# Sparse attention in a decoder trunk: normalising after the product with the values instead of before it

## The chip, the cores and the metric

The kernel runs on one core of one Trainium2 chip. The metric is the time of the whole program on the device, in microseconds (us): 1126.22 us is the median of three runs of the kernel before (1125.14, 1126.22 and 1126.79).

## What is computed

The reference is a two-layer decoder trunk for 512 tokens of 1024 channels. Layer 0 projects the normed tokens once and hands the columns to two mixers: gated linear attention, and a sparse attention with an indexer. An output projection, a gated convolutional FFN, a spatial gating layer and a second FFN follow. The change lies in the sparse attention, which, with the selection of keys already made, is

```python
s = einsum('bqhd,bqkd->bqhk', qb, kg) * d ** -0.5
s = where(valid[:, :, None, :], s, -inf)
p = softmax(s, axis=-1)
o = einsum('bqhk,bqkd->bqhd', p, vg)
```

for 8 heads of 64 channels; keys and values are shared by the heads. Since the softmax divides a row by one number, dividing the row of `o` instead of the row of `p` gives the same result.

## The kernel before, in words

Everything lies transposed, channels on the 128 partitions and tokens along the free axis, except where a step says otherwise. Weights come in chunks of 128 x 1024, each split in a high and a low part (`make_chunk`, lines 132 to 150), and a full-precision product is three matmuls (`mm3`, lines 159 to 162).

Layer 0 is cut into steps, and `ORDER` (lines 29 and 30) lists them in the order in which the scheduler prefers them. A scheduler then places the instructions on the engines: each engine runs its own list strictly in order, and a later step's instruction is put into a place where the scheduler sees the engine free. Its last steps are `W0 TC0 W3 A0 W1 W2 A3 A1 A2`, after which the output projection follows.

- `weigh(b)` (W, lines 509 to 527) takes 128 queries. For each of the 8 heads: two matmuls `ps_qk` (lines 296 and 297), a masked row with its minimum on VectorE (line 520), the exponential with the row's sum on ScalarE (line 522), the reciprocal of the sum (line 523), and the row times the reciprocal, on VectorE (line 525) or on ScalarE (line 527). `SWAPPED` names the rows that change places. Block b has 128 (b + 1) keys, so the rows of W0, W1, W2 and W3 are 128, 256, 384 and 512 wide.
- `gather(b)` (A, lines 529 to 547): for every 128 keys (`st`) and each half of the heads (`e`) four transposes `pt_p` (line 538), a copy `pT` to SBUF (line 541 on ScalarE or line 543 on VectorE, `SWAPPED` again), and the product with the values, `po` (line 545). The two halves write to partitions 0 to 63 and 64 to 127 of `po`. At the end `po` is split in two parts, `bh` on ScalarE (line 444) and `bl` on VectorE (line 445). That makes 2, 4, 6 and 8 copies for A0 to A3, 20 in all.
- `out_half` (lines 559 to 571) projects: first the half from the linear attention (`ah`, `al`; 8 tiles `p_o` of 12 matmuls each, 96 in all), then the half from the sparse attention (`bh`, `bl`; another 96), after which the next norm is prepared. The first half needs nothing from W and A.

PSUM has two pools of four tiles each: `pacc` (function `acc`) for the projections, and `paux` (function `aux`). A tile of a pool takes the place of the one allocated four before it. In the kernel before, `po` is an `aux` tile and the pool `pacc` holds only projections.

Of the kernel before, what the change touches and what calls it, by code (L numbers as in the profile page):

```python
# [10 lines left out]
AF = mybir.ActivationFunctionType  # L11
ALU = mybir.AluOpType
PSUM = bass.MemoryType.PSUM

P = 128
# [14 lines left out]
         "ST0 GL0 GL3 TC1 GL2 GL1 AR GT1 GT0 GT2 GT3 W0 TC0 W3 A0 W1 W2 A3 A1 A2")  # L30
MIX_LAG = 4
SPREAD = 3
# what GpSimd does in place of VectorE; where ScalarE and VectorE change places
ON_POOL = {
# [4 lines left out]
}  # L39
SWAPPED = {  # L40
# [3 lines left out]
}  # L44


# [1 line left out]
def trunk(ctx: ExitStack, tc: tile.TileContext, I, out):  # L48
    nc = tc.nc
    V, S, G, PE = nc.vector, nc.scalar, nc.gpsimd, nc.tensor  # L50
# [22 lines left out]
    def aux(name):  # L73
        return paux.tile([P, T], F32, tag="aux", name=name)

    # ---- inputs that stay
    pg = cst.tile([P, 40], F32, name="pg")
    nc.scalar.dma_start(pg, I["gains"])
    pv = cst.tile([P, I["pv"].shape[1]], F32, name="pv")
# [1 line left out]
    x = [xpool.tile([P, T], F32, tag="x", name=f"x{d}") for d in range(KD)]  # L81
    con = cst.tile([P, 3, P], F32, name="con")
    nc.gpsimd.dma_start(con, I["con"])
    ident, cmask, gmask = con[:, 0, :], con[:, 1, :], con[:, 2, :]
# [19 lines left out]
    one = cst.tile([P, 1], F32, name="one")  # L104
# [8 lines left out]
    mhalf = cst.tile([P, 4], F32, name="mhalf")  # L113
    V.memset(mhalf, -0.5)

    # ---- weights: loaded in chunks of [128, 1024], each split into two float32r parts
    order = []
    for name, n in (("w_in", 20), ("w_o", 8), ("w_up0", 44), ("w_dn0", 24), ("w_uv", 16),
                    ("w_out", 8), ("w_up1", 44), ("w_dn1", 24)):
# [41 lines left out]
        PE.matmul(ps, wh, xl, start=False, stop=False)  # L161
        PE.matmul(ps, wl, xh, start=False, stop=stop)  # L162

    # ---- the normed stream: x * gain in two parts, and 1/rms of each token
    class Normed:
        pass

# [21 lines left out]
            n.last = q  # L189

    def residual(d, ps, step):
        """x[d] += ps, then the next norm's step on it; the last one is what all wait for."""
        with tc.high_priority() if d == KD - 1 else nullcontext():
            V.tensor_add(x[d], x[d], ps)
            step(d)
# [25 lines left out]
        S.copy(n.R, pr)  # L221

    def chan(n, name):
        """A chunk's 128 channels by all tokens, before 1/rms."""
        wh, wl = chunk()
        ps = acc(name)
        for k in range(KD):
            c = slice(k * P, (k + 1) * P)
            mm3(ps, wh[:, c], wl[:, c], n.h[k], n.l[k], k == 0, k == KD - 1)
            if k == SPREAD and n.stage == 1:  # L230
                spread(n)
        if n.stage == 0:
            stats(n)
        return ps

    def tokens(n, name):
        """Four chunks' 512 channels, by blocks of tokens, before 1/rms."""
        ps = [acc(f"{name}{b}") for b in range(NB)]
        for c in range(4):
            wh, wl = chunk()  # L240
            for b in range(NB):
                t = slice(b * P, (b + 1) * P)
                for k2 in range(2):
                    k = 2 * c + k2
                    w = slice(k2 * T, (k2 + 1) * T)
                    PE.matmul(ps[b], n.h[k][:, t], wh[:, w], start=k == 0, stop=False)  # L246
                    PE.matmul(ps[b], n.l[k][:, t], wh[:, w], start=False, stop=False)  # L247
                    PE.matmul(ps[b], n.h[k][:, t], wl[:, w], start=False, stop=k == KD - 1)  # L248
            if n.stage == 0:
                stats(n)  # L250
        return ps

    # ---- layer 0: attention
    n0 = normed()
    ps = [(acc if j < 2 else aux)(f"p_first{j}") for j in range(4)]
    for c in range(4):
# [13 lines left out]
        nc.gpsimd.dma_start(CS[i], I["rope"][i])  # L270

    def halves(ps, cs, name):
        """A tile after its rotation, in two parts."""
        t1 = slot("rope1")
        sw = slot("rope2")
        t = slot("rope3")
        V.tensor_mul(t1, ps, cs[0])
        V.stream_shuffle(out=sw, in_=ps, mask=swap)
        eng("rm" + name).tensor_mul(sw, sw, cs[1])
        eng("ra" + name).tensor_add(t, t1, sw)  # L280
        h = slot("rope4", F32R)
        l = slot("rope5", F32R)
        S.copy(h, t)
        eng("rs" + name).tensor_sub(l, t, h)
        return h, l

    def queries(ps, cs, dst, name):
        """dst[e] = head e's high part over its low part."""
        h, l = halves(ps, cs, name)
        for e, rows in enumerate((lo, hi)):  # L290
            nc.sync.dma_start(dst[e][lo].bitcast(F32), h[rows].bitcast(F32))
            nc.sync.dma_start(dst[e][hi].bitcast(F32), l[rows].bitcast(F32))

    def dots(ps, q, ks):
        """All four products of the parts."""
        PE.matmul(ps, q, ks[0], start=True, stop=False)
        PE.matmul(ps, q, ks[1], start=False, stop=True)

# [8 lines left out]
    h, l = halves(ps[0], RCS, "kk")  # L307
# [44 lines left out]
                if picked[b] == TOPK // 8:  # L352
                    V.tensor_scalar(mask[b], mask[b], 0.5 * TAKEN, NEG, op0=ALU.is_gt, op1=ALU.mult)

    # gated linear attention
    def queries_keys(i):
        ps = ps_aq if i == 0 else chan(n0, f"p_qk{i}")
        if i < 2:
# [11 lines left out]
    def lazy(name, shape, dt=F32):  # L370
        if name not in B:
            B[name] = big(name, shape, dt)
        return B[name]
# [69 lines left out]
    def split(h, l, ps):  # L443
        S.copy(h, ps)
        V.tensor_sub(l, ps, h)
# [53 lines left out]
        split(lazy("ah", [P, 4, T], F32R)[:, :, t], lazy("al", [P, 4, T], F32R)[:, :, t],  # L499
              pt.rearrange("p (h c) -> p h c", c=P))  # L500

    # sparse attention
    def heads(i):
        bq = lazy(f"bq{i // 2}", [P, 4, T], F32R)
        queries(chan(n0, f"p_bq{i}"), RCS, [bq[:, 2 * (i % 2) + e, :] for e in range(2)], f"bq{i}")

    prob = {}

    def weigh(b):
        n = P * (b + 1)  # L510
        t = slice(b * P, (b + 1) * P)
        prob[b] = pr = [(big(f"pr{b}{e}", [P, 4, T]) if b else
                         slot(f"pr{b}{e}").rearrange("p (j t) -> p j t", t=P)) for e in range(2)]
        mx = small("mx", 8)
        sm = small("sm", 8)
        for h in (0, 2, 4, 6, 1, 3, 5, 7):
            p = pr[h % 2][:, h // 2, :n]
            ps = aux(f"ps_qk{b}{h}")
            dots(ps[:, :n], B[f"bq{h // 4}"][:, h % 4, t], [k[:, :n] for k in keys[1]])
            V.tensor_tensor_reduce(out=p, in0=ps[:, :n], in1=mask[b], op0=ALU.add, op1=ALU.min,  # L520
                                   scale=-0.125, scalar=3.0e38, accum_out=mx[:, h:h + 1])
            S.activation(p, p, AF.Exp, bias=mx[:, h:h + 1], scale=-1.0, accum_out=sm[:, h:h + 1])
            V.reciprocal(sm[:, h:h + 1], sm[:, h:h + 1])
            if (h % 2) != (f"nm{b}{h}" in SWAPPED):
                V.tensor_scalar(p, p, sm[:, h:h + 1], None, op0=ALU.mult)
            else:
                S.activation(p, p, AF.Copy, scale=sm[:, h:h + 1])

    def gather(b):
        t = slice(b * P, (b + 1) * P)  # L530
        pr = prob.pop(b)
        po = aux(f"po{b}")
        for st in range(b + 1):
            pT = []
            for e in range(2):
                pt = aux(f"pt_p{b}{st}{e}")
                for j in range(4):
                    PE.transpose(pt[:, j * P:(j + 1) * P], pr[e][:, j, st * P:(st + 1) * P], ident)
                pT.append(slot("pT"))
                if bool(e) != (f"pT{b}{st}{e}" in SWAPPED):  # L540
                    S.copy(pT[e], pt)
                else:
                    V.tensor_copy(pT[e], pt)
            for e in range(2):
                PE.matmul(po[64 * e:64 * e + 64, :], tok[:, st, 0:64], pT[e], start=st == 0, stop=st == b)  # L545
        split(lazy("bh", [P, 4, T], F32R)[:, :, t], lazy("bl", [P, 4, T], F32R)[:, :, t],
              po.rearrange("p (j c) -> p j c", c=P))

    picked = [0] * NB
    # the steps of layer 0 in the order that the scheduler prefers  # L550
    steps = {"QK": queries_keys, "SC": scores, "LG": logits, "DC": decays, "BQ": heads, "AV": values,
             "ST": states, "GL": gla, "AR": gates, "GT": gate, "W": weigh, "A": gather,
             "TC": lambda i: topk((1, 2, 3), 4)}
    for name in ORDER.split():
        step = steps[name.rstrip("0123")]
# [18 lines left out]
    n1 = normed()  # L574
    out_half(B["bh"], B["bl"], True, n1)

    # ---- gated conv FFN
    def ffn(l, n, nxt, gi):
        g = [big(f"g{l}_{i}", [P, 4, T], F32R) for i in range(NJ // 2)]
        for j in range(NJ):  # L580
# [48 lines left out]
                residual(d, ps, step)  # L629

    def close(n, ps, t):
        """The last residual, final norm and store of 256 tokens."""
        with tc.high_priority():
            xd = x[KD - 1][:, t]
            V.tensor_add(xd, xd, ps)
# [5 lines left out]
            for b in range(2):  # L641
                c = slice(b * P, (b + 1) * P)
# [6 lines left out]
            prs = []  # L649
# [6 lines left out]
            R = slot("R")[:, :256]  # L656
# [10 lines left out]
    n2 = normed()  # L667
    ffn(0, n1, n2, 1)

    # ---- layer 1: spatial gating  # L670
    v = [big(f"v{b}", [P, 2, T]) for b in range(NB)]
    for hh in range(2):
        ps = tokens(n2, f"p_v{hh}")
# [6 lines left out]
    for b in range(NB):  # L680
        st = small("bst", 12, 2).rearrange("p (a s) -> p a s", s=6)
# [35 lines left out]
    for g in range(8):  # L717
        ps = chan(n2, f"p_u{g}")
# [8 lines left out]
    for d in range(KD):  # L727
        wh, wl = chunk()
        ps = acc(f"p_so{d}")
# [8 lines left out]
def _layout(inp):  # L738
    import numpy as np

    f = {k: np.asarray(v) for k, v in inp.items()}
    A = {}
    A["xT"] = f["x"][0].T.reshape(KD, P, T)

    def by_k(w):
        """[K, n] -> [128, K / 128, n]"""
        return w.reshape(w.shape[0] // P, P, w.shape[1]).transpose(1, 0, 2)

    w = f["attn_w_in"][0]
# [31 lines left out]
    A["ln_b"] = f["sgu_ln_b"]  # L781
    A["b_s"] = f["sgu_b_s"][0].reshape(1, 1024)
    A["w_s"] = f["sgu_w_s"][0].transpose(2, 0, 1)
    # constants of the shapes
    i = np.arange(P)
    le = i[:, None] <= i[None, :]
    A["con"] = np.stack([np.eye(P, dtype=np.float32),
# [31 lines left out]
```

## Time and profile before

| | us |
|---|---|
| median of three runs | 1126.22 |
| span of the profiled execution | 1124.9 |
| TensorE (PE) busy in it | 1099.9 (98%) |
| VectorE (DVE) busy | 717.1 (64%) |
| ScalarE (ACT) busy | 451.2 (40%) |
| GpSimd (POOL) busy | 100.8 (9%) |

The span runs from the first to the last instruction; the runs' median is 1.3 us longer, which is what lies around it. A busy time of PE counts a matmul until its modelled end, so matmuls that follow one another overlap by a little. A row of the timeline gives the start and the duration; where a count stands behind it, the row is several instructions.

### The profile page before, as it was taken

The page shows a single profiled execution, that of the slowest core. Times are in us where ns is not written, and L with a number is a line of the kernel's source. Part 1 is how long each engine was busy: PE and PEld are TensorE (multiplying, and loading weights), DVE is VectorE, ACT ScalarE, POOL GpSimd, SP SyncE. Part 2 cuts the span into 40 slices and gives each one's busy share as a digit, 9 for nine tenths or more (in the row PEclk, how much of TensorE's full clock was granted, in tenths as well). Part 3 has the DMA queues.
Part 4 walks back from the last instruction along what each step waited for, and adds up shares of the span by engine and source line. Part 5 has one row for each costly group of instructions (what it writes and reads, how often), then busy time and mean ns, then how long its engine had stood idle before and what let it go on. Part 6 is the DMA issues. An engine that isn't in the chain of part 4 may idle for free.

```text
span 1124.9 us, 13026 instructions
## 1 busy us (share of the span) xinstructions
PE 1099.9 (98%) x5043; PEld 893.1 (79%) x5043; DVE 717.1 (64%) x1112; ACT 451.2 (40%) x649; POOL 100.8 (9%) x71
## 2 busy tenths in 40 slices
PE   8997999999999999999999999999999999999997
PEld 6875767487888888888888888888888888888886
DVE  5799789667777777753333385766777777753222
ACT  6452249144444444432222333435444444433221
POOL 1454240040000000000000000120000000000001
PEclk9998999999999999999999999999999999999999
DMA  6615120122222332223333523222233322233322
GB/s 225 187 38 150 57 68 9 38 94 94 94 94 95 103 102 95 94 85 103 99 94 108 169 75 113 76 94 94 94 96 104 100 94 94 94 103 87 101 85 75
DMA packets 34925, 108.86 MB, mean 97 GB/s; under 512 B 4160, under 2 KB 6480, under 8 KB 34864
## 3 DMA queue, kind: packets, MB, share of 16 engines
q1 hardware_dynamic: 33536, 104.87, 29.4%
q10 hardware_dynamic: 1040, 2.27, 0.7%
q8 instruction: 39, 0.64, 0.2%
q0 software_dynamic: 288, 0.90, 0.2%
q14 instruction: 22, 0.18, 0.0%
HBM read 101.73 MB, written 2.10 MB: 92 GB/s over the span
## 4 chain that ended last, share of the span: by engine, by line
PE 92%; DVE 5%; ACT 1%; issue 1%; DMA 0%; POOL 0%; POOLq 0%; SPq 0%; DVEq 0%; ACTq 0%
PE p_up L161 14%; PE p_up L162 14%; PE p_up L160 14%; PE p_dn L162 7%; PE p_dn L161 7%; PE p_dn L160 7%; PE po L545 1%; PE p_v L246 1%; PE p_so L160 1%; PE p_so L161 1%; PE p_u L160 1%; PE p_v L248 1%; PE p_u L161 1%; PE p_so L162 1%; PE p_u L162 1%; PE p_v L247 1%
## 5 line engine op out<-in xcount | busy, mean ns | idle before, releaser
L160 PE MATMUL p_up<-xh,h_w_up 128*128 128x512 f32 x704 | 274.3, 390 | 0.7 <-ACT xh L173 0.7
L161 PE MATMUL p_up<-xl,h_w_up 128*128 128x512 f32 x704 | 274.0, 389 | 0.6 <-DVE xl L174 0.6
L162 PE MATMUL p_up<-xh,l_w_up 128*128 128x512 f32 x704 | 273.9, 389 | 0.0
L160 PEld LDWEIGHTS p_up<-xh,h_w_up 128*128 128x128 f32 x704 | 132.1, 188 | 28.3 <-ACT xh L173 1.1
L161 PEld LDWEIGHTS p_up<-xl,h_w_up 128*128 128x128 f32 x704 | 132.1, 188 | 28.3 <-DVE xl L174 0.9
L162 PEld LDWEIGHTS p_up<-xh,l_w_up 128*128 128x128 f32 x704 | 132.1, 188 | 27.4
L161 PE MATMUL p_dn<-g,h_w_dn 128*128 128x512 f32 (+1 forms) x374 | 140.9, 377 | 0.0
L160 PE MATMUL p_dn<-g,h_w_dn 128*128 128x512 f32 (+1 forms) x374 | 140.9, 377 | 0.0
L162 PE MATMUL p_dn<-g,l_w_dn 128*128 128x512 f32 (+1 forms) x374 | 140.9, 377 | 0.0
L149 DVE TENSOR_TENSOR l_w_dn<-raw_w_dn,h_w_dn 128x1024 fp32r<-128x1024 f32 (+1 forms) x48 | 54.5, 1136 | 107.7 <-ACT h_w_dn L148 107.6
L148 ACT CAST h_w_up<-raw_w_up 128x1024 fp32r<-128x1024 f32 x88 | 92.7, 1054 | 62.5 <-PE p_up L161 47.7
L587 DVE TENSOR_TENSOR a<-p_up,R 128x512 f32<-128x512 f32 x88 | 60.5, 688 | 84.5 <-PE p_up L162 79.3
L149 DVE TENSOR_TENSOR l_w_up<-raw_w_up,h_w_up 128x1024 fp32r<-128x1024 f32 x87 | 106.5, 1224 | 9.4 <-ACT h_w_up L148 7.0
L148 ACT CAST h_w_dn<-raw_w_dn 128x1024 fp32r<-128x1024 f32 (+1 forms) x48 | 47.2, 983 | 147.8 <-PE p_dn L161 143.4
L160 PEld LDWEIGHTS p_dn<-g,h_w_dn 128*128 128x128 f32 x374 | 70.4, 188 | 13.0
L161 PEld LDWEIGHTS p_dn<-g,h_w_dn 128*128 128x128 f32 x374 | 70.4, 188 | 12.9
L162 PEld LDWEIGHTS p_dn<-g,l_w_dn 128*128 128x128 f32 x374 | 70.4, 188 | 12.8
L599 ACT CAST g<-c 128x512 fp32r<-128x512 f32 x44 | 27.3, 621 | 116.8 <-DVE c L596 116.8
L589 ACT ACTIVATE c<-a,pv 128x512 f32<-128x512 f32 x88 | 71.7, 815 | 2.9 <-DVE a L587 2.3
L592 DVE SCALAR_TENSOR_TENSOR c<-a,pv,c 128x510 f32<-128x510 f32 x88 | 65.9, 749 | 3.0
L590 DVE SCALAR_TENSOR_TENSOR c<-a,pv,c 128x511 f32<-128x511 f32 x88 | 65.6, 745 | 1.8 <-ACT c L589 1.8
L595 ACT ACTIVATE c<-c 128x512 f32<-128x512 f32 x44 | 27.8, 632 | 82.6 <-DVE c L592 82.6
(259 smaller groups left out, 1620.2 us busy)
## 6 DMA issues: line engine op xcount, KB each, us to landing
raw_w_up<-in_w_up SPq DMA_DIRECT2D x88, 512.0 KB, 3.3
raw_w_dn<-in_w_dn SPq DMA_DIRECT2D x32, 512.0 KB, 3.4
raw_w_in<-in_w_in SPq DMA_DIRECT2D x16, 512.0 KB, 3.6
raw_w_uv<-in_w_uv SPq DMA_DIRECT2D x16, 512.0 KB, 3.4
raw_w_dn<-in_w_dn SPq DMA_DIRECT2D x16, 384.0 KB, 3.1
raw_w_o<-in_w_o SPq DMA_DIRECT2D x8, 512.0 KB, 3.3
raw_w_out<-in_w_out SPq DMA_DIRECT2D x8, 512.0 KB, 3.4
x<-in_xT SPq DMA_DIRECT2D x8, 256.0 KB, 5.1
```

What stands on the lines that cost most here:

```text
L148: S.copy(h[:, :cols], raw[:, :cols])
L149: eng(name).tensor_sub(l[:, :cols], raw[:, :cols], h[:, :cols])
L160: PE.matmul(ps, wh, xh, start=start, stop=False)
L161: PE.matmul(ps, wh, xl, start=False, stop=False)
L162: PE.matmul(ps, wl, xh, start=False, stop=stop)
L246: PE.matmul(ps[b], n.h[k][:, t], wh[:, w], start=k == 0, stop=False)
L587: V.tensor_mul(a, ps, n.R)
L589: S.activation(cc, a, AF.Identity, bias=conv_b(l, m), scale=conv_w(l, m, 2))
L590: V.scalar_tensor_tensor(cc[:, 1:], a[:, :T - 1], conv_w(l, m, 1), cc[:, 1:], op0=ALU.mult, op1=ALU.add)
L592: V.scalar_tensor_tensor(cc[:, 2:], a[:, :T - 2], conv_w(l, m, 0), cc[:, 2:], op0=ALU.mult, op1=ALU.add)
L595: S.activation(c[0], c[0], AF.Silu)
L599: S.copy(gh, c[1])
```

## The change

- `weigh` leaves the probabilities as the exponentials. The 32 reciprocals of one column become 4 of eight columns, and the 32 multiplications of a row are gone.
- `gather` takes `po` from `acc` instead of `aux`. At its end GpSimd spreads the eight reciprocals over 512 columns (`wide`), PE transposes that in four pieces (`pt_rs`), ScalarE copies it to SBUF (`Rsum`), VectorE multiplies `o = po * Rsum`, and the split reads `o`.
- The copies `pT` go to VectorE for `e = 0` and to ScalarE for `e = 1`. `SWAPPED` is gone.

The diff without its removed comments:

```diff
-SWAPPED = {
...
-    prob = {}
+    prob, sums = {}, {}
...
             S.activation(p, p, AF.Exp, bias=mx[:, h:h + 1], scale=-1.0, accum_out=sm[:, h:h + 1])
-            V.reciprocal(sm[:, h:h + 1], sm[:, h:h + 1])
-            if (h % 2) != (f"nm{b}{h}" in SWAPPED):
-                V.tensor_scalar(p, p, sm[:, h:h + 1], None, op0=ALU.mult)
-            else:
-                S.activation(p, p, AF.Copy, scale=sm[:, h:h + 1])
+        V.reciprocal(sm, sm)
+        sums[b] = sm
...
         pr = prob.pop(b)
-        po = aux(f"po{b}")
+        rs = sums.pop(b)
+        po = acc(f"po{b}")
...
-                if bool(e) != (f"pT{b}{st}{e}" in SWAPPED):
+                if e:
                     S.copy(pT[e], pt)
                 else:
                     V.tensor_copy(pT[e], pt)
...
+        wide = slot("wide")
+        G.tensor_copy(wide.rearrange("p (h c) -> p h c", c=64), rs[:, :, None].to_broadcast([P, 8, 64]))
+        prs = aux(f"pt_rs{b}")
+        for j in range(4):
+            PE.transpose(prs[:, j * P:(j + 1) * P], wide[:, j * P:(j + 1) * P], ident)
+        R = slot("Rsum")
+        S.copy(R, prs)
+        o = slot("o")
+        V.tensor_mul(o, po, R)
         split(lazy("bh", [P, 4, T], F32R)[:, :, t], lazy("bl", [P, 4, T], F32R)[:, :, t],
-              po.rearrange("p (j c) -> p j c", c=P))
+              o.rearrange("p (j c) -> p j c", c=P))
```

The order of the instructions moves too. PE before, where A0 ends and W1 begins (`po0` is A0's product, `ps_qk1x` are W1's rows, `p_o1` and `p_o2` belong to the first half of the output projection):

```order
L160 MATMUL p_o1_1951<-ah_1447,h_w_o_0_1377 128x512
L545 MATMUL po0_1637<-pT_1643,tok_439 64x512
L296 MATMUL ps_qk10_1662<-key10_422,bq0_675 128x256
L545 MATMUL po0_1637<-pT_1650,tok_439 64x512
L297 MATMUL ps_qk10_1662<-key11_423,bq0_675 128x256
L296 MATMUL ps_qk12_1669<-key10_422,bq0_675 128x256
L297 MATMUL ps_qk12_1669<-key11_423,bq0_675 128x256
L296 MATMUL ps_qk14_1676<-key10_422,bq1_768 128x256
L297 MATMUL ps_qk14_1676<-key11_423,bq1_768 128x256
L161 MATMUL p_o1_1951<-al_1448,h_w_o_0_1377 128x512
L162 MATMUL p_o1_1951<-ah_1447,l_w_o_0_1378 128x512
```

PE in the changed kernel, the same place:

```order
L292 MATMUL ps_qk37_1601<-key11_423,bq1_768 128x512
L531 MATMUL pt_p000_1608<-con_91,pr00_1478 128x128 x4
L531 MATMUL pt_p001_1615<-con_91,pr01_1479 128x128 x4
L538 MATMUL po0_1607<-pT_1613,tok_439 64x512
L544 MATMUL pt_rs0_1626<-con_91,wide_1624 128x128
L538 MATMUL po0_1607<-pT_1620,tok_439 64x512
L544 MATMUL pt_rs0_1626<-con_91,wide_1624 128x128 x3
L291 MATMUL ps_qk10_1643<-key10_422,bq0_675 128x256
L292 MATMUL ps_qk10_1643<-key11_423,bq0_675 128x256
L291 MATMUL ps_qk12_1648<-key10_422,bq0_675 128x256
```

No `p_o` stands between the steps W and A any more. The first one stands near the end of A2, the last step (`po2` is its product):

```order
L538 MATMUL po2_1853<-pT_1882,tok_439 64x512
L531 MATMUL pt_p220_1886<-con_91,pr20_1684 128x128 x2
L531 MATMUL pt_p221_1893<-con_91,pr21_1685 128x128 x4
L155 MATMUL p_o0_1921<-ah_1447,h_w_o_0_1377 128x512
L156 MATMUL p_o0_1921<-al_1448,h_w_o_0_1377 128x512
L538 MATMUL po2_1853<-pT_1891,tok_439 64x512
L538 MATMUL po2_1853<-pT_1898,tok_439 64x512
L544 MATMUL pt_rs2_1904<-con_91,wide_1902 128x128 x4
L157 MATMUL p_o0_1921<-ah_1447,l_w_o_0_1378 128x512
```

All 96 of the first half stand from there on, without a break, and then the 96 of the second half. VectorE in the changed kernel, from W3's last row over A0's end to W1's first row:

```order
L515 ISA pr31_1563,mx_1564<-ps_qk37_1601,score3_533 128x512
L515 ISA mx_1564 128x1
L536 COPY pT_1613<-pt_p000_1608 128x512
L518 RECIPROCAL sm_1565<-sm_1565 128x8
L548 TENSOR_TENSOR o_1633<-po0_1607,Rsum_1631 128x512
L440 TENSOR_TENSOR bl_1636<-o_1633,bh_1635 128x4x128
L515 ISA pr10_1639,mx_1641<-ps_qk10_1643,score1_449 128x256
```

And ScalarE there, from W3's exponentials to W1's (before, ScalarE had only the split's `bh` between them):

```order
L517 ACTIVATE pr31_1563,sm_1565<-pr31_1563,mx_1564 128x512 x4
L534 COPY pT_1620<-pt_p001_1615 128x512
L546 COPY Rsum_1631<-pt_rs0_1626 128x512
L439 CAST bh_1635<-o_1633 128x4x128
L517 ACTIVATE pr10_1639,sm_1642<-pr10_1639,mx_1641 128x256 x4
```

So on all three engines W1 now stands behind the whole of A0. The products of the two halves, ten of which stood alone, stand side by side in A1, A2 and all but the first pair of A3. The instructions before W0 and those after the output projection's first half keep their order.

## Rows read from the trace of the kernel before

**Rows 1.** The page's span and busy times by engine.

```profile
span 1124.9 us, 13026 instructions
PE 1099.9 (98%) x5043; PEld 893.1 (79%) x5043; DVE 717.1 (64%) x1112; ACT 451.2 (40%) x649; POOL 100.8 (9%) x71
```

**Rows 2.** Busy us (x records): PE, PEld, DVE, ACT, POOL; PEclk; DMA share, GB/s.

```profile
168.20:228.40 60.20, 59.63 (x284) 38.46 (x283) 44.99 (x151) 30.41 (x86) 2.40 (x1) 1.00 0.09 29
205.00:210.00 5.00, 5.00 (x25) 2.23 (x25) 3.41 (x7) 0.59 (x1) 0.00 (x0) 1.00 0.09 35
```

**Rows 3.** Timeline of PE: first row of W0, first matmul of each next stage.

```profile
168.21 0.30 PE L296 MATMUL ps_qk<-key,bq 128*128 128x128 f32 x1
...
228.36 0.39 PE L160 MATMUL p_o<-bh,h_w_o 128*128 128x512 f32 x1
...
250.12 0.39 PE L160 MATMUL p_up<-xh,h_w_up 128*128 128x512 f32 x1
```

**Rows 4.** Groups of W and A, by line (168 to 228.4 us): what is removed or moved.

```profile
L543 DVE COPY pT<-pt_p 128x512 f32<-128x512 f32 x19 | 12.8, 685 | 5.0 <-PE pt_p L538 4.9
L525 DVE TENSOR_SCALAR pr<-pr,sm 128x256 f32<-128x256 f32 (+3 forms) x21 | 8.1, 393 | 0.0
L527 ACT ACTIVATE pr<-pr,sm 128x128 f32<-128x128 f32 (+3 forms) x11 | 5.7, 516 | 0.1
L523 DVE RECIPROCAL sm<-sm 128x1 f32<-128x1 f32 x32 | 4.7, 156 | 0.9 <-ACT pr L522 0.7
```

**Rows 5.** The exponentials by width, and the load of their table.

```profile
L522 ACT ACTIVATE pr<-pr,mx 128x512 f32<-128x512 f32 x8 | 5.6, 708 | 0.0
L522 ACT ACTIVATE pr<-pr,mx 128x384 f32<-128x384 f32 x8 | 4.8, 604 | 0.0
L522 ACT ACTIVATE pr<-pr,mx 128x256 f32<-128x256 f32 x8 | 4.0, 500 | 0.4 <-DVE mx L520 0.3
L522 ACT ACTIVATE pr<-pr,mx 128x128 f32<-128x128 f32 x8 | 3.1, 388 | 0.0
170.09 1.28 ACT L522 ACT_TABLE_LOAD   x1 [1.01 <-DVE mx L520]
```

**Rows 6.** Timeline, PE: products alone and in pairs, transposes between and behind them.

```profile
181.33 1.07 PE L545 MATMUL po<-pT,tok 128*64 128x512 f32 x2
182.33 0.38 PE L296 MATMUL ps_qk<-key,bq 128*128 128x256 f32 x1
197.66 1.08 PE L545 MATMUL po<-pT,tok 128*64 128x512 f32 x4
198.67 1.53 PE L538 MATMUL pt_p<-con,pr 128*128 128x128 f32 x12
199.96 0.48 PE L162 MATMUL p_o<-ah,l_w_o 128*128 128x512 f32 x1
```

**Rows 7.** Timeline, ACT and DVE: the parts of the hand-over, W1's first row, the last exponential.

```profile
181.87 0.67 DVE L571 TENSOR_TENSOR x<-x,p_o 128x512 f32<-128x512 f32 x1
183.75 0.59 ACT L444 CAST bh<-po 128x512 fp32r<-128x512 f32 x1 [0.84 <-PE po L545]
184.38 0.69 DVE L445 TENSOR_TENSOR bl<-po,bh 128x512 fp32r<-128x512 f32 x1 [0.85 <-ACT bh L444]
184.98 0.42 DVE L520 CUSTOM_DVE_ANT_0 pr<-ps_qk,score 128x256 f32<-128x256 f32 x1
197.00 0.60 ACT L522 ACTIVATE pr<-pr,mx 128x384 f32<-128x384 f32 x1
212.03 0.59 ACT L541 COPY pT<-pt_p 128x512 f32<-128x512 f32 x1 [3.82 <-PE pt_p L538]
```

**Rows 8.** GpSimd's dearest group of 128x512.

```profile
L306 POOL TENSOR_TENSOR rope_rs<-rope_s,R 128x512 f32<-128x512 f32 x1 | 1.7, 1741 | 0.0
```

**Rows 9.** Busy time by stretch: a sparse stretch of PE, and the one behind it.

```profile
96.90:100.80 3.90, 0.50 (x1) 0.19 (x1) 3.90 (x7) 0.47 (x1) 3.90 (x2) 0.90 0.53 126
100.83:106.94 6.11, 6.11 (x15) 4.79 (x15) 6.11 (x20) 1.67 (x2) 3.90 (x4) 0.50 0.70 226
```

More of the change, by code (lines that the diff above doesn't have):

```diff
@@ L38 @@
     "w_in_4", "w_in_8", "w_o_0", "w_o_1", "w_o_5", "w_up0_1",
-}
-SWAPPED = {
[3 rows of a table removed]
 }
```

3 rows, old and new, of the table SWAPPED are left out of this document.

## The prediction

> **What bounds the kernel now.** I read the page first. PE is busy for 98% of the span, DVE for 64%, ACT for 40% [rows 1], so work taken off DVE or ACT pays only where PE waits for it. Then the stretch that the change touches, from W0's first matmul at 168.21 to the first matmul of the second half of the output projection at 228.36 [rows 3]: 60.15 us. PE is busy for 59.6 of 60.2 us there, at a granted clock of 1.00, DVE for 45.0 and ACT for 30.4 [rows 2]. The reader is to see that PE has no gap in this stretch. Where W and A leave it free, it runs the first half of the output projection: 96 matmuls at (250.12 - 228.36) / 96 = 0.227 us [rows 3], 21.8 us in all, which the order of before spreads among W's and A's instructions.
>
> **What the change takes off and puts on, engine by engine.** DVE loses 21 multiplications (8.1 us), 28 of 32 reciprocals (4.1) and 9 of 19 copies (9 x 0.685 = 6.2) [rows 4], and gains four products `o` (4 x 0.67, as the addition from PSUM [rows 7]): -15.7 us. ACT loses 11 multiplications (5.7) [rows 4], and gains 9 copies and four `Rsum` (13 x 0.59 [rows 7]): +2.0 us. GpSimd gains four copies `wide`. Their price isn't in the trace; its dearest operation of that size took 1.74 us [rows 8], and even a copy of that length is hidden: A0's starts behind W0's sums, some 3 us before its transposes, A2's some 15 us before. Were it twice as long, A0 alone would wait, for under 1 us. PE gains 16 transposes at (199.96 - 198.67) / 12 = 0.108 us: +1.7. It loses something too: a product of one half takes 1.00 us, and two side by side take 1.01 [rows 6]. Before, 5 pairs and 10 single ones make 15 us; now 8 pairs and 4 single ones make 12: -3.0. By sums of work alone, PE has 1.3 us less to do, and nothing speaks for a slower kernel.
>
> **What moves, and where the time goes.** The order decides. `po` now takes its place in the pool of the projections, ahead of their tiles; the orders shown have no `p_o` between W and A, and all 96 behind A2's transposes. So the 21.8 us that filled the gaps now follow the gaps. I add the stretch up again, from the load of the exponentials' table, which ends at 171.37 as before [rows 5], since nothing earlier moves.
>
> 1. W0 and W3. PE has two matmuls a row, DVE one operation of 0.67 us at most; the exponentials are the slowest of the three: 8 x 0.388 + 8 x 0.708 = 8.8 us [rows 5]. They end at 180.1.
> 2. The hand-over to W1, a wait that was not there. ACT has A0's second copy behind W3's exponentials, PE has A0's second product in front of W1's matmuls, DVE has `o` and `bl` in front of W1's first row. In a chain: copy 0.59, product 1.00, the three transposes left and their latency 0.6, `Rsum` 0.59, `o` 0.67, `bh` 0.59, `bl` 0.69, first row of W1 0.42 [rows 6, 7], with eight hand-overs of 0.04 (183.75 + 0.59 to 184.38): 5.5 us. W1's exponentials begin at 185.6. Queued behind that: all of W1 and W2.
> 3. W1 and W2: 8 x 0.500 + 8 x 0.604 = 8.8 us [rows 5]. The last exponential ends at 194.4; before, it ended at 197.6 [rows 7].
> 4. A3, A1, A2. When ACT turns to A3's copies at 194.4, PE has four to five transposed groups and one product behind it. Left are 13 groups of four transposes (13 x 0.43 = 5.6), one single product and 8 pairs (9.1), three times `pt_rs` (1.3), and ten changes from product to transpose at some 0.16: 17.6 us. To this come PE's waits for copies: between nothing, if the four `aux` tiles let the transposes run ahead, and 9 x (0.2 + 0.69) = 8 us, if each pair waits for its copies in full. The tiles hold two pairs, so I take 3 us: the first pair, which waits for ACT, and the start of each gather. PE is through at 215.0.
> 5. The first half of the output projection, without cover: 96 x 0.227 = 21.8. The second half starts at 236.8.
>
> That is 236.8 - 228.4 = 8.4 us later than before. What follows keeps its order. Its weights are loaded and split while step 5 runs: each chunk waits for the matmuls of the chunk three before it, and is needed two chunks, 48 x 0.227 = 10.9 us, later. So it takes as long as before. The sum against the profiled span is 1124.9 + 8.4 = 1133.3 us; with the 1.3 us by which the runs' median stands above the span, **1134.7 us**. The unknowns: the waits of step 4 give -3 to +5, and a slow clock once, +3 (below). This case's own range is 1131.5 to 1142.7.
>
> **The clock.** PE's gaps now lie between W's rows. In the stretch 96.9 to 100.8 PE had 0.5 us of work, and the next 6.1 us ran at a granted clock of 0.50, 1.2 GHz, half the speed [rows 9]: some 3 us lost. In W a half clock costs little, as ACT is slower than PE either way; at the start of step 4 it would cost up to 3 us. I count it in the range only: the longest gap that the steps leave on PE is in step 2, where W1's matmuls have filled the four `aux` tiles and wait for `o`, `bh`, `bl` and W1's first row, at most 0.67 + 0.59 + 0.69 + 0.42 = 2.4 us.
>
> **The rivals.**
>
> *A slow clock through the whole of A (9%).* If the clock falls in W and comes back only with the `p_o` matmuls, step 4 runs at half speed: another 16 us of PE's work, less the 3 us of waits that then vanish, +13: 1148 us. For it: A is now nothing but transposes and products of half width. Against it: from 205 to 210 us PE ran those alone but for one `p_o`, and the granted clock stayed at 1.00 [rows 2]. It had been high before, though; that it rises in such a stretch no row shows. The Trainium skill (TensorE: Matmul & The Clock Gate, Part 4: PE-mode transpose) says that the full clock doesn't engage for transposes, which don't count as work in the same way. By that, this rival would be the likely one; the stretch from 205 to 210 us speaks against it.
>
> *Faster (7%).* The chain of weighing sets the end, not PE. The last exponential ends at 194.4 instead of 197.6, 3.2 us earlier, and DVE has 15.7 us less. If PE had slack behind that point, the stretch would end 3.2 us earlier: 1123.0 us. It decides if less than 3 us of PE's work is left uncovered. For it: ACT was busy 11.2 of 12 us from 172 to 184, just the stretch where it also normalised. Against it: PE has no gap in rows 2, and the order leaves 21.8 us uncovered.
>
> *No difference (6%).* The lost cover costs next to nothing. Of the 60.15 us before, PE's work accounts for less than all (21.8 for `p_o`, 8.6 for transposes, 15 for products, some 10 for W's 64 matmuls: 56), so some 4 us of waits were there already, counted as busy, and the new ones may be as short. If the hand-over of step 2 shrinks to under 1 us (-5) and step 4 never waits (-3), 8.4 - 8 leaves 1126.6 us. It needs both, and each part of the hand-over reads the one before it.
>
> **How the numbers follow.** The forecast has 78%, the slow clock through A 9%, faster 7%, no difference 6%. The range, 1130 to 1142.5, reaches from between the forecast's lower end and no difference to the forecast's upper end, and leaves out the two far rivals and a part of the third. A measurement of this kernel can tell 0.2%, 2.3 us, from no change. Faster by more: the second rival, 7%. Within: the third, 6%. Slower: the forecast and the slow clock, 87%.
>
> **What would show it.** In the profile after: a busy share of PE well under one from 168 to 195 us; W1's first row about 5 us behind W3's last exponential, on ACT and DVE; the last exponential near 194.4; the products mostly in pairs; 96 `p_o` of the first half in one block of 21.8 us; the second half starting near 237. DVE's total falls by some 16 us and nothing comes of it. The forecast is wrong if `p_o` matmuls fill the gaps after all, if the hand-over takes under 2 us, or if the granted clock is near 0.50 from 195 to 215 us.

## The result, and the profile after

The changed kernel takes 1134.81 us, the median of four runs (1134.3 to 1136.43), and the kernel before 1126.11 us beside it (four runs, 1125.14 to 1126.79). The ratio is 1.0084, with a 95% interval of 1.0071 to 1.0098: slower by about 0.8%, as forecast.

The page of the changed kernel, its span and busy times by engine; it answers to [rows 1].

```profile
span 1132.6 us, 13025 instructions
PE 1103.8 (97%) x5059; PEld 899.2 (79%) x5059; DVE 707.1 (62%) x1058; ACT 453.6 (40%) x651; POOL 105.1 (9%) x75
```

DVE's total fell by 10.0 us and the span rose by 7.7 us. PE's total rose although it has less to do, for PE counts matmuls that wait for each other, or run at half clock, as busy. So I look at the stretch again, from W0's first matmul to the first matmul of the second half of the output projection, now 164.50 to 232.43. By stretch, for the changed kernel, with the columns of [rows 2]; the second row is A without A0:

```profile
164.50:232.45 67.95, 63.74 (x300) 45.27 (x299) 34.78 (x97) 32.80 (x88) 4.85 (x5) 0.92 0.08 26
191.00:211.00 20.00, 19.40 (x105) 10.01 (x105) 7.25 (x12) 7.18 (x15) 1.23 (x2) 1.00 0.01 1
```

The stretch takes 67.93 us instead of 60.15 [rows 3]: 7.8 us longer. DVE is busy for 34.8 instead of 45.0 us in it, ACT for 32.8 instead of 30.4 [rows 2]. In the second row the granted clock is 1.00, so A did not run slowly.

The timeline of the changed kernel, all engines: the load of the exponentials' table, the hand-over from W3 and A0 to W1, and ACT's first copies behind W2's exponentials.

```profile
166.38 1.28 ACT L517 ACT_TABLE_LOAD   x1 [1.01 <-DVE mx L515]
...
175.71 0.70 ACT L517 ACTIVATE pr<-pr,mx 128x512 f32<-128x512 f32 x1
176.41 0.56 ACT L534 COPY pT<-pt_p 128x512 f32<-128x512 f32 x1
...
177.35 1.07 PE L538 MATMUL po<-pT,tok 128*64 128x512 f32 x2
178.35 0.55 PE L544 MATMUL pt_rs<-con,wide 128*128 128x128 f32 x3
...
178.94 0.59 ACT L546 COPY Rsum<-pt_rs 128x512 f32<-128x512 f32 x1 [1.97 <-PE pt_rs L544]
...
179.63 0.69 DVE L548 TENSOR_TENSOR o<-po,Rsum 128x512 f32<-128x512 f32 x1 [2.89 <-ACT Rsum L546]
...
180.35 0.62 ACT L439 CAST bh<-o 128x512 fp32r<-128x512 f32 x1 [0.83 <-DVE o L548]
...
181.00 0.69 DVE L440 TENSOR_TENSOR bl<-o,bh 128x512 fp32r<-128x512 f32 x1 [0.68 <-ACT bh L439]
181.61 0.42 DVE L515 CUSTOM_DVE_ANT_0 pr<-ps_qk,score 128x256 f32<-128x256 f32 x1
...
182.09 0.39 PE L291 MATMUL ps_qk<-key,bq 128*128 128x256 f32 x1 [2.01 <-DVE mx L515]
182.13 0.51 ACT L517 ACTIVATE pr<-pr,mx 128x256 f32<-128x256 f32 x1 [1.16 <-DVE mx L515]
...
191.02 1.05 ACT L534 COPY pT<-pt_p 128x512 f32<-128x512 f32 x2
```

The reader is to follow the chain from row to row: ACT's copy, A0's second product, `pt_rs`, `Rsum`, `o`, `bh`, `bl`, W1's first row, W1's first exponential. From the end of W3's last exponential to W1's first it is 182.13 - 176.41 = 5.7 us. PE stands idle for 2.0 us at the end of it, as the bracket says, with nothing left to put in.

The other end, PE's timeline of the changed kernel: pairs of products in A, A2's last transposes, and the first matmul of the second half.

```profile
201.62 1.94 PE L538 MATMUL po<-pT,tok 128*64 128x512 f32 x8 [0.25 <-DVE pT L536]
...
206.14 1.94 PE L538 MATMUL po<-pT,tok 128*64 128x512 f32 x8
...
210.61 0.66 PE L544 MATMUL pt_rs<-con,wide 128*128 128x128 f32 x4
211.03 0.48 PE L157 MATMUL p_o<-ah,l_w_o 128*128 128x512 f32 x1
...
232.43 0.39 PE L155 MATMUL p_o<-bh,h_w_o 128*128 128x512 f32 x1
```

From 211.03 to 232.43 PE runs the first half of the output projection in one block of 21.4 us.

To see where PE's time went, I give each row of PE's timeline the time to the start of the next row, and add up by tile, for before, after and three kernels of the experiments below (us):

| PE's time at | before | after | e1_aux | e2_acc | r2_b1 |
|---|---|---|---|---|---|
| `ps_qk` (W, 64 matmuls) | 11.6 | 19.1 | 11.1 | 20.8 | 10.9 |
| `pt_p` (80 transposes) | 8.9 | 11.6 | 9.2 | 12.5 | 8.7 |
| `po` (20 products, in 40 records) | 15.3 | 13.2 | 14.3 | 16.2 | 12.7 |
| `pt_rs` (16 transposes) | 0 | 2.0 | 2.0 | 0 | 1.9 |
| `p_o` (96 matmuls) | 24.3 | 22.1 | 24.0 | 21.9 | 24.0 |
| the stretch | 60.15 | 67.93 | 60.6 | 71.4 | 58.2 |

Before to after: W's matmuls take 7.5 us more, since PE now waits between them with nothing to do. `po` gives back 2.1 us, because the halves are paired, and `pt_rs` takes that again. The rows of A's transposes, with the waits behind them, take 2.7 us more, and the `p_o` matmuls, in one block, save 2.2 us of changes. Together 7.8 us.

### The profile page after: what moved, and what is told of

Read it like the earlier page. It is cut to its first block, busy times and chain, and to the rows that moved or that the text cites. A ratio compares the mean times of both kernels' runs of the same rounds, so it can differ in the third digit from the quotient of the medians.

```text
span 1132.6 us, 13025 instructions
## 1 busy us (share of the span) xinstructions
PE 1103.8 (97%) x5059; PEld 899.2 (79%) x5059; DVE 707.1 (62%) x1058; ACT 453.6 (40%) x651; POOL 105.1 (9%) x75
## 4 chain that ended last, share of the span: by engine, by line
PE 60%; issue 32%; DVE 5%; ACT 1%; DMA 1%; POOL 1%; SPq 0%; POOLq 0%; DVEq 0%; ACTq 0%
PE p_up L156 7%; PE p_up L157 7%; PE p_up L155 7%; PE p_dn L157 4%; PE p_dn L156 4%; PE p_dn L155 4%; PE p_so L155 1%; PE p_v L241 1%; PE p_u L155 1%; PE p_so L156 1%; PE p_v L243 1%; PE p_u L157 1%; PE p_v L242 1%; PE p_u L156 1%; PE p_so L157 1%
```

## Experiments

Two theories stood against each other. By the first, the loss is that of the cover: `po` asks for its tiles ahead of `p_o`, so nothing fills PE's gaps any more. By the rival, it is the added work: `wide`, `pt_rs`, `Rsum` and `o` lengthen a chain on which the end depends.

**r1_after: the changed kernel once more.**

> The changed kernel once more, unaltered, for a second profile. In the first one the stretch from W0's first matmul to the second half of the output projection took 67.9 us (before: 60.15), and the spells of half clock lay elsewhere than in the profile of before: two fewer ahead of W0 (3.7 us gained), one more behind the output projection at 261 us (3.3 us lost). If the longer stretch is the change's own, it is again 67 to 69 us. If the spell at 261 us belongs to the change, it is there again at the same place, and W0 starts near 164.5 us; if the spells fall by chance, they lie elsewhere. Time 1133 to 1137 us either way.

Measured: 1133.66 us (1132.12 to 1136.49), ratio 1.0075 (1.0059 to 1.0091). The loss repeats. The stretch took 67.6 us. W0 starts at 164.5 us again, and the spell at half clock behind the output projection is there again too, at 262 us and half as long; the last section returns to it.

**e1_aux: one line of the change undone.** All added work stays.

```diff
-        po = acc(f"po{b}")
+        po = aux(f"po{b}")
```

> The changed kernel with po taken from aux again, nothing else; the order then has p_o matmuls between the rows of W and A as before. Theory of the lost cover: the stretch falls from 67.9 us to 58 to 61 us, since PE has 1.3 us less work than before and its gaps are filled, and the time is 1124 to 1128 us. Rival, that the added work (the spread sums, their transposes and copies, the hand-over between the engines) costs the time: all of it is still there, the stretch stays at 66 us or more, and the time stays above 1133 us.

Measured: 1126.02 us, ratio 1.0006 (0.9996 to 1.0016). By stretch, for this kernel:

```profile
165.30:225.90 60.60, 59.98 (x300) 40.24 (x299) 34.21 (x97) 32.99 (x88) 4.96 (x5) 1.00 0.09 29
```

PE is full again (59.98 of 60.60 us), with the same DVE and ACT work as in the changed kernel. So the whole loss hangs on that one line. It also shows what the rest of the change is worth in time while PE is covered: nothing that can be told. The 11 us that DVE is spared were time in which PE had other work.

**e2_acc: that one line alone, put into the kernel before.**

```diff
-        po = aux(f"po{b}")
+        po = acc(f"po{b}")
```

> The kernel before with po taken from acc, nothing else: it normalises as before and adds no work. Theory of the lost cover: the 96 matmuls of the first half stand behind A2 again, the stretch grows from 60.15 us to 66 to 71 us, and the time is 1132 to 1138 us. Rival, added work: nothing was added, 1126 us and 60 us.

Measured: 1138.07 us (1135.33 to 1142.16), ratio 1.0115 (1.0092 to 1.0138), at the upper end of what the theory gave. By stretch, and PE's timeline behind A2, for this kernel:

```profile
168.20:239.60 71.40, 64.89 (x284) 39.03 (x283) 45.35 (x151) 30.67 (x86) 2.39 (x1) 1.00 0.08 24
```

```profile
216.69 1.07 PE L545 MATMUL po<-pT,tok 128*64 128x512 f32 x2
217.69 0.50 PE L160 MATMUL p_o<-ah,h_w_o 128*128 128x512 f32 x1
...
239.59 0.39 PE L160 MATMUL p_o<-bh,h_w_o 128*128 128x512 f32 x1
```

The block of 21.9 us is there without any of the added work, and the stretch is 11.2 us longer than before. Beside the changed kernel it is 3.5 to 3.8 us longer: without cover the multiplications and single products stand on the path, and only then is the rest of the change worth something. The table has it: `po` 16.2 against 13.2 us, `ps_qk` 20.8 against 19.1, `pt_p` 12.5 against 11.6, less 2.0 for `pt_rs`. How much of it belongs to the multiplications and how much to the even split of the copies, no run separates.

**e3_a0late: the changed kernel with A0 behind W1.**

```diff
-... W0 TC0 W3 A0 W1 W2 A3 A1 A2")
+... W0 TC0 W3 W1 A0 W2 A3 A1 A2")
```

> The changed kernel with A0 behind W1 in ORDER instead of in front of it. The chain from A0's second copy to W1's first row then no longer stands between W3 and W1, but between W1 and W2, where it is as long. Theory of the hand-over: the row that waits is W2's first instead of W1's, so the gap of about 5 us moves there and the time changes by less than 2 us (1133 to 1137 us). If instead the gap is only there because PE, DVE and ACT all come to A0 right behind the long rows of W3, the gap shrinks and 2 to 4 us come back: 1130 to 1133 us.

Measured: 1134.75 us, ratio 1.0081 (1.0068 to 1.0094), no gain. ACT's timeline for this kernel, from W1's last exponential to W2's first:

```profile
183.71 0.49 ACT L517 ACTIVATE pr<-pr,mx 128x256 f32<-128x256 f32 x1
184.11 0.19 ACT L517 ACTIVATION_READ_ACCUMULATOR pr<-pr,mx 128x1 f32 x1
184.21 0.56 ACT L534 COPY pT<-pt_p 128x512 f32<-128x512 f32 x1
...
186.41 0.59 ACT L546 COPY Rsum<-pt_rs 128x512 f32<-128x512 f32 x1 [1.64 <-PE pt_rs L544]
...
187.82 0.62 ACT L439 CAST bh<-o 128x512 fp32r<-128x512 f32 x1 [0.83 <-DVE o L548]
...
189.80 0.62 ACT L517 ACTIVATE pr<-pr,mx 128x384 f32<-128x384 f32 x1 [1.36 <-DVE mx L515]
```

The wait is the same, 189.80 - 184.21 = 5.6 us, one step later.

**e4_nonorm: the changed kernel without the added steps**, `po` left where the change put it.

```diff
-        wide = slot("wide")
...
-        V.tensor_mul(o, po, R)
...
-              o.rearrange("p (j c) -> p j c", c=P))
+              po.rearrange("p (j c) -> p j c", c=P))
```

> The changed kernel without `wide`, `pt_rs`, `Rsum` and `o`: the results of the product with values are split as they are, so the division by the sums is left out; `po` stays in the pool of the projections. All 96 matmuls of the first half of the output projection still follow A2's transposes. Theory: the lost cover costs 21.8 us of matmuls in one block, and the added steps stand on the path as well, as PE has nothing else to do: without them W1 need not wait for A0 (its first matmuls now stand ahead of A0's product), which takes some 5 us off, and three `pt_rs` with their changes (3 x 0.59 us) go from A: 1134.3 - 6.8 = about 1127.5 us. Rival: the hand-over is one of several waits that cover for each other (moving A0 behind W1 gained nothing), so only the transposes go: about 1132.5 us.

Measured: 1132.88 us (1131.35 to 1133.36), ratio 1.0066 (1.0048 to 1.0083): near the rival's 1132.5, not my 1127.5. But the rival's reason did not hold either, as the rows show. ACT's timeline from the hand-over on, and PE's in A (four records are a pair of products), for this kernel:

```profile
177.49 0.57 ACT L534 COPY pT<-pt_p 128x512 f32<-128x512 f32 x1
179.64 0.59 ACT L439 CAST bh<-po 128x512 fp32r<-128x512 f32 x1 [1.59 <-PE po L538]
181.38 0.51 ACT L517 ACTIVATE pr<-pr,mx 128x256 f32<-128x256 f32 x1 [1.16 <-DVE mx L515]
...
190.16 1.05 ACT L534 COPY pT<-pt_p 128x512 f32<-128x512 f32 x2
```

```profile
201.90 1.38 PE L538 MATMUL po<-pT,tok 128*64 128x512 f32 x4
203.22 0.66 PE L531 MATMUL pt_p<-con,pr 128*128 128x128 f32 x4
203.80 1.82 PE L538 MATMUL po<-pT,tok 128*64 128x512 f32 x4
...
210.76 0.50 PE L155 MATMUL p_o<-ah,h_w_o 128*128 128x512 f32 x1
```

The hand-over shrinks from 5.7 to 181.38 - 177.49 = 3.9 us, no further: the split into `bh` and `bl` still stands ahead of W1's rows on DVE, and it waits for the product. In A nothing is gained at all. From W2's last exponential to the block of `p_o` it is 210.76 - 190.16 = 20.6 us, against 211.03 - 191.02 = 20.0 in the changed kernel. There two pairs of products ran in 1.94 us, 0.97 each; here a pair takes 1.38 or 1.82, as it catches up with its copies, with fewer transposes in between. So `pt_rs` was not a cost in A: it filled waits. The whole stretch, from 165.45 to 232.66, is 67.2 us, only 0.4 to 0.7 us shorter than in the changed kernel's two profiles. So the added steps account for less than 1 of the 7.8 us, and that the time came so near the rival's is luck.

**e5_split: the even split of the copies alone, in the kernel before** (the names beginning with pT struck from `SWAPPED`).

```diff
-    "nm24", "nm25", "nm30", "nm32", "nm33", "nm34", "pT001", "pT101", "pT111",
-    "pT200", "pT201", "pT211", "pT221", "pT301", "pT311", "pT321", "pT331",
+    "nm24", "nm25", "nm30", "nm32", "nm33", "nm34",
```

> The kernel before with one part of the change alone: the copies of the transposed probabilities split evenly, DVE the even and ACT the odd half; the multiplications by the reciprocals stay. DVE loses 9 copies (6.2 us), ACT gains 9 (5.3 us). Theory: PE sets the pace and 26 instead of 28 matmuls of the first half are left behind A2, so no difference that can be measured: 1125.8 us, within 1.2. Rival: ACT's copies stand behind its exponentials and multiplications, and PE waits for them: 1 to 2 us slower, 1127 to 1128.

Measured: 1125.5 us, ratio 1.0005 (0.9994 to 1.0016). No difference, as expected.

**e6_own and e7_acc5: whose turn, or how many tiles?** The first gives `po` a pool of its own with one tile. The second leaves it where it is and adds a tile there. Both take a tile from the transposes.

```diff
-    paux = ctx.enter_context(tc.tile_pool(name="paux", bufs=4, space=PSUM))
+    paux = ctx.enter_context(tc.tile_pool(name="paux", bufs=3, space=PSUM))
+    ppo = ctx.enter_context(tc.tile_pool(name="ppo", bufs=1, space=PSUM))
...
-        po = acc(f"po{b}")
+        po = ppo.tile([P, T], F32, tag="po", name=f"po{b}")
```

```diff
-    pacc = ctx.enter_context(tc.tile_pool(name="pacc", bufs=4, space=PSUM))
-    paux = ctx.enter_context(tc.tile_pool(name="paux", bufs=4, space=PSUM))
+    pacc = ctx.enter_context(tc.tile_pool(name="pacc", bufs=5, space=PSUM))
+    paux = ctx.enter_context(tc.tile_pool(name="paux", bufs=3, space=PSUM))
```

> The changed kernel with `po` in a pool of its own with one tile, and three tiles instead of four for the transposes. 48 matmuls of the first half are left uncovered behind A2 (96 in the changed kernel, 36 with `po` in the pool of four). Theory: what costs the time is that `po` asks for its tiles ahead of `p_o` in the pool of the projections; with `po` out of there the gaps fill again, and the time is back at 1126, up to 2 us more for the one tile that A's steps hand on. Rival: A needs four tiles for its transposes, and PE waits for copies with three: 1130 us or more.

> The changed kernel with five tiles in the pool of the projections and three for the transposes. `po` still asks first, and 94 matmuls of the first half still follow A2. Theory: the order of the requests decides, not the number of tiles: as the changed kernel, 1134 us, up to 3 more for the tile that the transposes lose. Rival: the pool was too small for both; with a fifth tile the time falls by 3 us or more, to 1131 or less.

Measured: e6_own 1132.77 us, ratio 1.0062 (1.0047 to 1.0077); e7_acc5 1137.55 us, the median of three executions (1137.21 to 1138.88; the fourth is in the last section), ratio 1.0107 (1.0091 to 1.0122). The fifth tile brings no gain, as the theory had it. The time is some 3 us above the changed kernel's, about the most that the theory allowed for the tile that the other pool lost; where these 3 us lie, its profile can't show. For e6_own the time was the rival's, but its place was not. By stretch, and PE's first row of W0, for e6_own:

```profile
171.25:232.70 61.45, 60.79 (x299) 40.26 (x297) 34.11 (x97) 32.91 (x88) 4.85 (x5) 1.00 0.10 31
```

```profile
171.25 0.33 PE L292 MATMUL ps_qk<-key,bq 128*128 128x128 f32 x1
```

The stretch is 61.45 us, within 1.3 us of before: the gaps are filled. But it begins 3.0 us later than before [rows 3]. That time is lost in the linear attention, whose tiles come from the pool of three as well. PE's timeline there, for the kernel before and then for e6_own:

```profile
120.82 0.60 PE L424 MATMUL ps_kt<-con,ka 128*128 128x128 f32 x4
...
125.05 1.09 PE L430 MATMUL ps_ds<-av,kt 64*64 64x128 f32 x28
```

```profile
120.45 0.60 PE L420 MATMUL ps_kt<-con,ka 128*128 128x128 f32 x4
...
128.19 0.87 PE L426 MATMUL ps_ds<-av,kt 64*64 64x128 f32 x12
```

At `ps_kt` e6_own is still 0.4 us ahead. Each of the two sets of states then holds one `ps_kt` tile and two `ps_ds` tiles. Before, the 28 records of the second set run together; in e6_own the last 12 of them come 3.1 us later, and the last output `ps_o` begins 5.5 us later (155.80 against 150.27). The granted clock is 1.00 in both from 107 us to W0, so it is not a matter of the clock. So the pool of three costs the time, as the rival said, but in other steps than A. Where the 1.4 us lie by which the median stands above the profiled execution (1131.39 us), no profile shows.

**b1_order, b2_order, b3_norm: can the order of the steps beat both kernels?** b1 and b2 are e1_aux with another order; b3 is e5_split with b1's. b1 was run a second time as r2_b1.

```diff
-... W0 TC0 W3 A0 W1 W2 A3 A1 A2")
+... W0 TC0 W3 W1 W2 A3 A0 A1 A2")
```

```diff
-... W0 TC0 W3 A0 W1 W2 A3 A1 A2")
+... W0 TC0 W3 A0 W1 A1 W2 A2 A3")
```

> The changed kernel with `po` back in the pool of four and the steps in the order W0 W3 W1 W2 A3 A0 A1 A2. Theory: what counts is how many matmuls of the first half of the output projection are left uncovered behind the last A: 17 here, 36 with `po` back and the old order of the steps. 19 x 0.227 = 4.3 us less behind A2, a part of it given back where they displace no wait: about 1123 us. Rival: PE is full in the whole stretch either way, and the matmuls only change places: 1126 us.

> The changed kernel with `po` back in the pool of four and the steps in the order W0 W3 A0 W1 A1 W2 A2 A3. Theory: A1's copies and transposes lie beside W2's exponentials; 31 matmuls of the first half are left uncovered instead of 36, 1.1 us: about 1125 us. Rival: A1's copies stand in ACT's and DVE's queues ahead of W2 and delay its exponentials, as A0 delays W1: 1127 us or more.

> The kernel before with the copies split evenly and the steps in the order W0 W3 W1 W2 A3 A0 A1 A2, the multiplications left in. PE has no `pt_rs` (1.9 us less than in the kernel with the same order and unnormalised probabilities), but 40 matmuls of the first half are left behind A2 there. Theory: PE is full in the whole stretch, so its own work decides: 58.2 - 1.9 = 56.3 us for the stretch, and 1122 to 1124 us. Rival: W's exponentials and multiplications set its pace (ACT), the A steps without cover wait for their copies: 1126 us or more.

> The kernel with `po` back in the pool of four and the order W0 W3 W1 W2 A3 A0 A1 A2 once more. Its stretch was 58.2 us against 60.15 before, but its profiled run had a spell at half clock in the projections behind it. If the 2 us hold, it is 0.1 to 0.2% faster than before; if not, no difference.

Measured: b1 1125.73 us, ratio 0.9999 (0.9986 to 1.0011), and again 1124.89 us, 0.9994 (0.9985 to 1.0003); b2 1128.53 us, 1.0026 (1.0013 to 1.0038); b3 1124.53 us, 0.9987 (0.9978 to 0.9996). By stretch, for r2_b1, and then for b3_norm:

```profile
164.10:222.30 58.20, 57.59 (x299) 40.04 (x298) 33.66 (x97) 32.68 (x88) 4.76 (x5) 1.00 0.11 35
```

```profile
167.70:227.70 60.00, 58.54 (x283) 39.08 (x282) 39.30 (x142) 35.16 (x95) 2.39 (x1) 1.00 0.10 29
```

b1's stretch is 58.2 us both times, 2.4 us shorter than e1_aux's, where the `p_o` matmuls taken from behind A2 add up to 4.3. In the timed runs it can't be told from before. Both of its profiles have a spell at half clock in the FFN (last section) that the kernel before hasn't: from the second half's first matmul to the end they take 898.4 and 900.1 us, against 896.5 before. In those profiles that takes back the 2 us. b3 is perhaps 0.1% faster; my 56.3 us for its stretch was wrong: `po` took 14.9 us there, not 12.7. b2 is slower: A1 does stand in W2's way, whose last matmul comes at 198.1 there, at 188.4 in e1_aux. None of them beats the kernel before by as much as 0.2%.

## Why the prediction was right

Its case was the right one, and its steps can be checked one by one. The table of the exponentials was loaded 3.7 us earlier in the profile after (it ends at 166.38 + 1.28 = 167.66 instead of 171.37 [rows 5]), so durations are compared:

| step | predicted | measured |
|---|---|---|
| 1. W0 and W3, exponentials | 8.8 | 176.41 - 167.66 = 8.8 |
| 2. the hand-over to W1 | 5.5 | 182.13 - 176.41 = 5.7 |
| 3. W1 and W2, exponentials | 8.8 | 191.02 - 182.13 = 8.9 |
| 4. A3, A1, A2 | 20.6 | 211.03 - 191.02 = 20.0 |
| 5. the first half of the projection | 21.8 | 232.43 - 211.03 = 21.4 |
| stretch, against before | +8.4 | +7.8 |

Step 4 held its 3 us of waits nearly in full (20.0 less 17.6 is 2.4), but e4_nonorm says that its terms don't simply add: the 1.3 us for `pt_rs` would have come back as waits for copies. In step 5 two matmuls had slipped in before A2's last products. What follows took as long as before, as the prediction had it: from the second half's first matmul to the end, the eight profiles without a spell at half clock there took 896.5 to 896.8 us, the kernel before among them.

The total agrees to 0.1 us, which is better than the reasons were and so in part luck. Against the predicted span of 1133.3 us, the stretch is 0.6 us too short, its start 3.7 us earlier (two spells at half clock ahead of it, where the profile before has four), a spell at half clock in the FFN adds 3.3 us (below), the rest 0.3 us: 1132.6 us. And what lies around the span was 2.1 us (1134.7 - 1132.6 for the profiled execution), where I took 1.3: that set the median of three runs beside the span of one of them. In e3_a0late W0 starts at 168.2 as before, there is no such spell, and span and stretch grow alike, by 7.6 us each.

**The signs.** Two came otherwise than the prediction said. DVE's total fell by 10.0 us, not by some 16. Summed over its groups, DVE's work in the stretch did fall as forecast, from 54.4 to 38.8 us; but rows that follow each other on DVE overlap, and the busy time counts such a piece once (45.0 and 34.8 us), so a sum of rows is more than what the page will show. And PE's busy share was not well under one in W: 22.9 of 26.5 us from 164.5 to 191.0, part of it at half clock. In e3_a0late, at a granted clock of 1.00, it was 19.8 of 26.6 us from 168.2 to 194.8, which is what the sign meant. Two small sums of the prediction were off, without weight for the forecast: PE's work in the *no difference* rival adds up to 55.4 us, not 56, and the low end of its own range is 1134.7 - 3 = 1131.7.

**The price not seen** was GpSimd's `wide`. The group in the changed kernel:

```profile
L541 POOL COPY wide<-sm 128x512 f32<-128x512 f32 x4 | 2.5, 614 | 36.9 <-PE po L538 21.1 <-DVE sm L518 8.8 <-DVE o L548 7.0
```

It took 0.61 us each, a third of the bound of 1.74, and nothing waited for it.

**The rivals.** *Faster* (the chain of weighing sets the end): the last exponential did end earlier, 191.02 - 167.66 = 23.4 us behind the table's load instead of 26.2 [rows 5, 7], and DVE was relieved, but the end of the stretch came later. *No difference* (the hand-over shrinks, A never waits): both waits were there. *A slow clock through the whole of A*: the clock fell to 0.50 in W, from 166 to 173 and from 183 to 187 us, as the prediction feared, and yet A ran at 1.00. The stretch from 191 to 211 us holds transposes and products of half width and hardly anything else. The clock had come back in W2's matmuls, at 186.8 us, and stayed. The Trainium skill (TensorE: Matmul & The Clock Gate, Part 4: PE-mode transpose) says that the full clock doesn't engage for transposes. That did not decide here: A has products beside its transposes, and its granted clock was 1.00. Whether it would have risen within A no run here shows. W's spells cost nothing that I can find: e3_a0late, with a granted clock of 1.00 in its whole stretch, took 67.7 us, as long as the 67.6 and 67.9 of the two runs with spells.

## What to carry to other kernels

A pool of tiles is also a queue. A tile that asks ahead of others in the pool of the fill-in work shuts that work out, even when the change is about something else; look at what the full engine runs in its gaps before you count what another engine saves. Work taken off an engine that isn't the bound was worth nothing here while the gaps were filled, and some 3.5 us once they were not (the stretch of e2_acc beside the changed kernel's). And a wait taken out of a chain of waits is worth what the next one leaves: twice (e4_nonorm, b1_order) the sum promised more than the chip gave.

## What the runs showed of the hardware

The same instructions, with the same gaps, do not always keep their clock. At the start of the FFN, PE waits for the normed stream. By stretch, for e1_aux and then for r2_b1, PE's busy time, and the granted clock third from the end:

```profile
252.10:253.60 1.50, 0.73 (x4) 0.23 (x2) 1.50 (x2) 1.19 (x2) 0.00 (x0) 1.00 0.00 0
253.60:255.10 1.50, 0.88 (x5) 0.54 (x4) 0.81 (x2) 0.05 (x1) 0.00 (x0) 1.00 0.66 153
255.10:256.60 1.50, 1.50 (x12) 1.41 (x11) 0.57 (x2) 1.00 (x1) 0.33 (x1) 1.00 0.49 197
```

```profile
248.60:250.10 1.50, 0.72 (x3) 0.19 (x1) 1.50 (x2) 1.12 (x2) 0.00 (x0) 1.00 0.00 0
250.10:251.60 1.50, 0.88 (x5) 0.62 (x5) 0.74 (x2) 0.12 (x1) 0.00 (x0) 1.00 0.67 147
251.60:253.10 1.50, 1.50 (x10) 1.50 (x9) 0.14 (x2) 0.92 (x1) 0.00 (x0) 0.55 0.50 202
253.10:254.60 1.50, 1.50 (x4) 1.15 (x4) 1.16 (x2) 0.00 (x0) 1.40 (x1) 0.50 0.00 0
```

Both gaps leave PE 1.6 of 3.0 us of work; behind one the clock stays at 1.00 (2.4 GHz), behind the other it falls to 0.50 (1.2 GHz) for some 7 us, which costs some 3.5 us. The changed kernel's profile has such a spell there, from 261.8 to 268.6 us, and the one before has none; that is the 3.3 us above. It fell in five of the thirteen profiles read: both of the changed kernel, both of b1_order, and e4_nonorm. In two of them it lasted some 7 us, in three some 3.5; from the second half's first matmul to the end these took 900.1 to 900.2 and 898.2 to 898.4 us, the eight others 896.5 to 896.8. Both kernels that were profiled twice had it both times, if not for as long, so it may hang on the kernel's order or may have fallen by chance; these runs don't decide it. A profile that differs by 2 to 4 us at such a place is therefore read stage by stage.

e7_acc5 showed the extreme: in its profiled execution the granted clock lay near 0.50 from 127 to 175 us, and it took 1158.57 us. No stage is read from that profile.
